# A hybrid decoder block: a fourth pair of the gate/up product by seven products, SiLU in one activation, unsplit feed-forward blocks

## The chip, the cores and the metric

The kernel runs on one core of one Trainium2 chip. The metric is the device time of one execution in microseconds (us), lower is better. TensorE (PE) multiplies, VectorE (DVE) and ScalarE (ACT) work elementwise, GpSimd (POOL) issues a few DMAs, SyncE (SP) issues the loads of weights.

## The reference

One decoder layer on 256 tokens of width 2048, in float32. The part around the change is the SwiGLU feed-forward:

```python
    x = x + jnp.concatenate([attn_out, mlstm_out], axis=-1) @ w_out[i]
    h2 = rms_norm(x, w_norm_ffn[i])
    x = x + (jax.nn.silu(h2 @ w_ffn_gate[i]) * (h2 @ w_ffn_up[i])) @ w_ffn_down[i]
    gate = jax.nn.sigmoid(rms_norm(x, w_norm_ple[i]) @ w_ple_gate[i])
    e = rms_norm(p[i] @ w_ple_proj[i], w_ple_post_norm[i])
    x = x + gate * e
```

Ahead of it stand attention and an mLSTM with their projections. The feed-forward is 5632 wide.

## The kernel before

Every float32 product is made of three: both factors are split into a high part (`h`, rounded to the matmul's format) and a low part (`l`, what is left), and h·h, h·l and l·h are added up in PSUM. `halves` splits weights: ACT writes the high part (`wh`, line 219), DVE subtracts (`wl`, line 220). On a tile of 128x1024 elements each is one instruction.

The gate and up projections run over 11 columns of 512 features (`gate_up`). A column needs the 256 tokens (two blocks of 128) times 16 blocks of the inner dimension, taken as eight pairs. For one pair, token blocks x inner blocks and inner blocks x (gate, up) are two 2x2 matrices of blocks, so a pair is eight block products (`plain_unit`, 24 matmuls) or, by the scheme of Strassen and Winograd, seven (`seven_unit`, 21 matmuls). Seven products need sums of blocks: DVE makes four sums of weights per pair (`wt`, lines 731 to 735), and these are split too (`th`, `tl`; the same two lines 219 and 220). The sums of token blocks are made once for each pair (`make_forms`, tiles `fh`, `fl`). The tuple `seven` names the pairs done so, `later_order` the order of the eight pairs in columns 1 to 10. Column 0 has a tuple and an order of its own.

At a column's end eight additions on DVE (lines 780 to 789) combine the banks of PSUM; then comes SiLU: ACT takes a sigmoid (line 793), DVE multiplies twice (lines 794, 795). `after_up` turns the block round: DVE transposes 32x32 pieces (line 187), POOL sends it to memory and back (`swap`, `quad`), and ACT copies it out. The blocks of columns 0 to 3 are split there at once into a high and a low part (lines 129, 130); those of columns 4 to 10 are kept in float32 (line 668) and split by `split_raw` each time that the down projection (`linear` on `w_down`, four columns of 512, called from `residual`) comes to one.

The order of instructions on each engine is that of a scheduler, which moves them within the order of the code by its own estimate. An engine works its list off in order. Loads of weights go through SP into four buffers `wr`; `wh` and `wl` have four buffers each, `wt`, `th` and `tl` two.

Of the kernel before, what the change touches and what calls it, by code (L numbers as in the profile page):

```python
# [14 lines left out]
P = 128  # L15
# [4 lines left out]
def block_kernel(ctx, tc, x, p, w_norm_mix, w_in, fox_f_bias, q_norm_w, k_norm_w, conv_w, conv_b,  # L20
# [202 lines left out]
    def linear(w, acts, c0, n, pieces=None, before=None, load=None, width=2, split_raw=None):  # L223

        acts = list(acts)
        po = [ps.tile([P, 512], F32, name=f"acc{b}") for b in range(2)]
        total = w.shape[0] // P
        if pieces is None:
            step = 1024 // n if n < 512 else 2
            pieces = [(k, min(step, total - k)) for k in range(0, total, step)]  # L230
        count = 0
        ready = []

        def fetch(i):
            kt, nk = pieces[i]
            if load is not None:
                load(kt)

            ready.append(halves(load_piece(w, kt, nk, c0, n)))

        for i, (kt, nk) in enumerate(pieces):
            if before is None:
                advance(width)
                fetch(i)
            else:
                if i == 0:
                    fetch(0)
                    before(kt)
                if i + 1 < len(pieces):
                    fetch(i + 1)  # L250
                if i:
                    before(kt)
            wh, wl = ready[i]
            for j in range(nk):
                ah, al = acts[(kt + j) // 4]
                while id(ah) in made_by and not made_by[id(ah)].done:
                    advance(2)
                if al is None:
                    ah, al = acts[(kt + j) // 4] = split_raw(ah)
                kk = (kt + j) % 4  # L260
                count += 1
                for b in range(2):
                    s = slice(b * P, (b + 1) * P)
                    nc.tensor.matmul(po[b][:, 0:n], ah[:, kk, s], wh[:, j, :], start=count == 1, stop=False)  # L264
                    nc.tensor.matmul(po[b][:, 0:n], ah[:, kk, s], wl[:, j, :], start=False, stop=False)  # L265
                    nc.tensor.matmul(po[b][:, 0:n], al[:, kk, s], wh[:, j, :], start=False, stop=count == total)  # L266
        return [t[:, 0:n] for t in po]


# [389 lines left out]
    with tc.tile_pool(name="ffnp", bufs=1) as fp:  # L659
        acts_g = []  # L660

        def after_up(dst, gg):
            if dst[1] is not None:
                yield from split_by_blocks(dst, lambda b: gg[b])
                return
            tv = yield from transposed(lambda b: gg[b])
            for k in range(0, 4, 2):
                nc.scalar.copy(dst[0][:, k:k + 2].rearrange("p k (t r) -> p k t r", r=32), tv[:, k:k + 2])
                if not k:
                    yield  # L670
            held.pop()
# [7 lines left out]

        first_seven, seven = (1, 2), (1, 2, 4)
        first_order, later_order = (0, 3, 4, 1, 5, 2, 6, 7), (0, 3, 1, 5, 2, 6, 4, 7)
        forms = {}

        def make_forms(p):
# [58 lines left out]
        def gate_up(c):  # L745

            own, shared = (("acc0", "acc1"), ("tr", "sc"))[::1 - 2 * (c % 2)]
            tags = {"P1": own[0], "P6": own[0], "P7": own[1], "P5": own[1],
                    "P2": shared[0], "P3": shared[1], "P4": shared[0], "P8": shared[1]}
            order, by_seven = (later_order, seven) if c else (first_order, first_seven)  # L750
            n7 = len(by_seven)
            left = {**{n: n7 for n in ("P1", "P6", "P7", "P5")}, **{n: 16 - n7 for n in ("P2", "P3", "P4")}, "P8": 16 - 2 * n7}
            bank, t1, qr, su = {}, None, None, None
            for p in order:
                advance(1)
                if p in by_seven:
                    while p not in forms:
                        advance(1)
                    unit = seven_unit(c, p)
                else:  # L760
                    h = acts_h[p // 2]
                    unit = plain_unit(c, p, h)
                    while id(h[0]) in made_by and not made_by[id(h[0])].done:
                        advance(2)
                advance(1)
                for n, (lh, ll), (rh, rl) in unit:
                    first = n not in bank
                    if first:
                        bank[n] = ps.tile([P, 512], F32, name=tags[n])
                    left[n] -= 1  # L770
                    nc.tensor.matmul(bank[n], lh, rh, start=first, stop=False)  # L771
                    nc.tensor.matmul(bank[n], lh, rl, start=False, stop=False)  # L772
                    nc.tensor.matmul(bank[n], ll, rh, start=False, stop=left[n] == 0)  # L773
                if su is None and left["P1"] == 0:
                    while held:
                        advance(1)
                    t1 = fp.tile([P, 512], F32, name="sg", bufs=2)
                    nc.scalar.copy(t1, bank["P1"])
                    qr = quads.tile([P, 2, 512], F32, name="quad")
                    nc.vector.tensor_tensor(qr[:, 0], bank["P6"], t1, op=ALU.add)  # L780
                    nc.vector.tensor_tensor(qr[:, 1], bank["P7"], qr[:, 0], op=ALU.add)
                    su = quads.tile([P, 2, 512], F32, name="tq")
                    for i in range(2):
                        nc.vector.tensor_tensor(su[:, i], bank["P5"], qr[:, i], op=ALU.add)
            gg = [fp.tile([P, 512], F32, name=f"gg{b}") for b in range(2)]
            nc.vector.tensor_tensor(gg[0], bank["P2"], t1, op=ALU.add)
            nc.vector.tensor_tensor(gg[1], bank["P4"], qr[:, 1], op=ALU.add)
            nc.vector.tensor_tensor(su[:, 0], bank["P3"], su[:, 0], op=ALU.add)
            nc.vector.tensor_tensor(su[:, 1], bank["P8"], su[:, 1], op=ALU.add)
            for b in range(2):  # L790
                r = rstd2[:, b:b + 1]
                sg = fp.tile([P, 512], F32, name="sg", bufs=2)
                nc.scalar.activation(sg, gg[b], AF.Sigmoid, scale=r)
                nc.vector.scalar_tensor_tensor(gg[b], gg[b], r, sg, op0=ALU.mult, op1=ALU.mult)
                nc.vector.scalar_tensor_tensor(gg[b], su[:, b], r, gg[b], op0=ALU.mult, op1=ALU.mult)
            return gg

        for c in range(NG):
# [1 line left out]
                Task(make_forms(kp), [made_by[id(acts_h[kp // 2][0])]])  # L800
            gg = gate_up(c)
            if c < 4:
                acts_g.append(new_act())
            else:
                acts_g.append((fp.tile([P, 4, 256], F32, name=f"g{c}"), None))
            made_by[id(acts_g[c][0])] = Task(after_up(acts_g[c], gg))
# [84 lines left out]
```

## Time and profile before

| | |
|---|---|
| time, median of 3 runs | 1218.33 us (1216.01 to 1219.6) |
| the profiled execution's own time | 1218.38 us |
| its span from the first to the last instruction | 1216.6 us |
| PE busy | 1201.3 us, 99% of the span |
| DVE busy | 918.6 us, 76% |
| ACT busy | 669.1 us, 55% |

Busy times of PE overlap one another, since matmuls are pipelined: what one matmul takes is read from the distance between two starts, not from its own duration. The same holds, to a smaller degree, for DVE.

### The profile page before, as it was taken

The page shows a single profiled execution, that of the slowest core. Times are in us where ns is not written, and L with a number is a line of the kernel's source. Part 1 is how long each engine was busy: PE and PEld are TensorE (multiplying, and loading weights), DVE is VectorE, ACT ScalarE, POOL GpSimd, SP SyncE. Part 2 cuts the span into 40 slices and gives each one's busy share as a digit, 9 for nine tenths or more (in the row PEclk, how much of TensorE's full clock was granted, in tenths as well). Part 3 has the DMA queues.
Part 4 walks back from the last instruction along what each step waited for, and adds up shares of the span by engine and source line. Part 5 has one row for each costly group of instructions (what it writes and reads, how often), then busy time and mean ns, then how long its engine had stood idle before and what let it go on. Part 6 is the DMA issues. An engine that isn't in the chain of part 4 may idle for free.

```text
span 1216.6 us, 15632 instructions
## 1 busy us (share of the span) xinstructions
PE 1201.3 (99%) x5579; PEld 999.1 (82%) x5579; DVE 918.6 (76%) x1270; ACT 669.1 (55%) x884; POOL 79.7 (7%) x149
## 2 busy tenths in 40 slices
PE   9999999999999999999999999999999999999998
PEld 6899978888888787787788878887788888888888
DVE  5767755656656999899999999998965757565854
ACT  6655556547545646455555555565554645456542
POOL 1111000001010000000000000000000000000000
PEclk9999999999999999999999999999999999999999
DMA  7677744676577676676776777676676666664772
GB/s 262 208 237 234 239 139 125 185 231 191 190 246 238 200 226 198 225 232 192 235 232 202 245 217 231 204 251 216 210 249 207 207 211 206 218 209 161 236 229 88
DMA packets 136386, 257.33 MB, mean 212 GB/s; under 512 B 10003, under 2 KB 29301, under 8 KB 136309
## 3 DMA queue, kind: packets, MB, share of 16 engines
q1 hardware_dynamic: 127156, 229.06, 59.2%
q0 software_dynamic: 8400, 26.22, 6.8%
q8 instruction: 43, 0.70, 0.2%
q10 hardware_dynamic: 752, 1.06, 0.2%
q14 instruction: 35, 0.28, 0.1%
HBM read 241.10 MB, written 15.20 MB: 211 GB/s over the span
## 4 chain that ended last, share of the span: by engine, by line
PE 83%; DVE 6%; DMA 6%; issue 2%; ACT 1%; POOL 1%; SPq 0%; DVEq 0%; POOLq 0%; ACTq 0%
PE acc L265 18%; PE acc L266 18%; PE acc L264 18%; PE acc L772 5%; PE acc L773 5%; PE acc L771 5%; DMA quad<-swap 3%; DMA swap<-tq 2%; PE tr L772 2%; PE tr L773 2%; PE tr L771 2%; PE sc L772 2%; PE sc L773 2%; PE sc L771 2%; DVE wl L220 2%
## 5 line engine op out<-in xcount | busy, mean ns | idle before, releaser
L220 DVE TENSOR_TENSOR wl<-wr,wh 128x1024 fp32r<-128x1024 f32 (+2 forms) x445 | 504.4, 1142 | 189.8 <-ACT wh L219 188.8
L219 ACT CAST wh<-wr 128x1024 fp32r<-128x1024 f32 (+2 forms) x445 | 433.8, 986 | 330.5 <-PE acc L266 204.2
L264 PE MATMUL acc<-wh,act_h 128*128 128x512 f32 (+2 forms) x864 | 320.1, 371 | 0.6 <-ACT act_h L133 0.5
L266 PE MATMUL acc<-wh,act_l 128*128 128x512 f32 (+2 forms) x864 | 318.0, 368 | 0.0
L265 PE MATMUL acc<-wl,act_h 128*128 128x512 f32 (+2 forms) x864 | 317.5, 368 | 0.4 <-DVE wl L220 0.4
L264 PEld LDWEIGHTS acc<-wh,act_h 128*128 128x128 f32 x864 | 162.8, 188 | 24.9 <-ACT act_h L133 1.3
L266 PEld LDWEIGHTS acc<-wh,act_l 128*128 128x128 f32 x864 | 162.7, 188 | 24.5 <-DVE act_l L135 0.8
L265 PEld LDWEIGHTS acc<-wl,act_h 128*128 128x128 f32 x864 | 162.9, 189 | 23.6 <-DVE wl L220 0.9
L191 POOL DMA_DIRECT2D swap<-tq x100 | 61.2, 618 | 867.5 <-DVE tq L187 832.1
L219 ACT CAST th<-wt 128x1024 fp32r<-128x1024 f32 x64 | 67.2, 1051 | 72.2 <-DVE wt L732 63.4
L771 PE MATMUL acc<-wh,act_h 128*128 128x512 f32 x232 | 90.3, 390 | 0.7 <-ACT wh L219 0.7
L773 PE MATMUL acc<-wh,act_l 128*128 128x512 f32 x232 | 90.6, 390 | 0.0
L772 PE MATMUL acc<-wl,act_h 128*128 128x512 f32 x232 | 90.5, 390 | 0.0
L266 PE MATMUL acc<-wh,tl 128*128 128x512 f32 x224 | 87.2, 390 | 1.1 <-DVE tl L220 1.1
L265 PE MATMUL acc<-wl,th 128*128 128x512 f32 x224 | 88.1, 393 | 0.0
L264 PE MATMUL acc<-wh,th 128*128 128x512 f32 x224 | 87.9, 393 | 0.0
L220 DVE TENSOR_TENSOR tl<-wt,th 128x1024 fp32r<-128x1024 f32 x64 | 78.0, 1221 | 5.2 <-ACT th L219 4.9
L772 PE MATMUL tr<-wl,act_h 128*128 128x512 f32 x156 | 61.0, 391 | 0.6 <-DVE wl L220 0.6
L773 PE MATMUL tr<-wh,act_l 128*128 128x512 f32 x156 | 61.0, 391 | 0.0
L771 PE MATMUL tr<-wh,act_h 128*128 128x512 f32 x156 | 60.6, 390 | 0.0
L220 DVE TENSOR_TENSOR tl<-g,th 128x1024 fp32r<-128x1024 f32 x28 | 34.3, 1223 | 24.5 <-ACT th L219 24.4
L771 PEld LDWEIGHTS acc<-wh,act_h 128*128 128x128 f32 x232 | 43.6, 188 | 10.4 <-ACT wh L219 1.1
(285 smaller groups left out, 1495.9 us busy)
## 6 DMA issues: line engine op xcount, KB each, us to landing
wr<-in_w_ffn_gate_dram SPq DMA_DIRECT2D x88, 512.0 KB, 3.5
wr<-in_w_ffn_up_dram SPq DMA_DIRECT2D x88, 512.0 KB, 4.6
wr<-in_w_ffn_down_dram SPq DMA_DIRECT2D x88, 512.0 KB, 4.7
wr<-in_w_in_dram SPq DMA_DIRECT2D x63, 512.0 KB, 4.8
wr<-in_w_in_dram SPq DMA_DIRECT2D x48, 344.0 KB, 3.9
wr<-in_w_out_dram SPq DMA_DIRECT2D x32, 512.0 KB, 4.1
wr<-in_w_ple_gate_dram SPq DMA_DIRECT2D x32, 512.0 KB, 4.5
swap<-tq POOLq DMA_DIRECT2D x100, 128.0 KB, 3.8
```

The source lines that it names most:

```text
L191: nc.gpsimd.dma_start(out=d[:, :, :, i, :].rearrange("j c b e -> c b j e"), in_=t[32 * i:32 * i + 32].rearrange("c b j k r -> c b j (k r)"))
L219: nc.scalar.copy(wh, wr)
L220: nc.vector.tensor_tensor(wl, wr, wh.bitcast(F32), op=ALU.subtract)
L264: nc.tensor.matmul(po[b][:, 0:n], ah[:, kk, s], wh[:, j, :], start=count == 1, stop=False)
L265: nc.tensor.matmul(po[b][:, 0:n], ah[:, kk, s], wl[:, j, :], start=False, stop=False)
L266: nc.tensor.matmul(po[b][:, 0:n], al[:, kk, s], wh[:, j, :], start=False, stop=count == total)
L771: nc.tensor.matmul(bank[n], lh, rh, start=first, stop=False)
L772: nc.tensor.matmul(bank[n], lh, rl, start=False, stop=False)
L773: nc.tensor.matmul(bank[n], ll, rh, start=False, stop=left[n] == 0)
```

## The change

There are three edits and a new order. Pair 5 joins the pairs done by seven products in columns 1 to 10, and the order of the pairs there becomes 0, 1, 3, 2, 4, 6, 5, 7. ACT computes SiLU itself, and one multiplication on DVE goes. The blocks of columns 0 to 3 stay in float32 as the others do, so that the down projection splits all eleven each time it comes to them. For that, `linear` gets the function `ahead`, which issues the split of the next group of four blocks one group early, and `after_up` waits three steps of background work, not two, between its transfers.

```diff
     def linear(w, acts, c0, n, pieces=None, before=None, load=None, width=2, split_raw=None):
         acts = list(acts)
+
+        def ahead(k):
+
+            raw = acts[k // 4][0]
+            if acts[k // 4][1] is None and (id(raw) not in made_by or made_by[id(raw)].done):
+                acts[k // 4] = split_raw(raw)
+
...
+            if split_raw is not None and kt % 4 == 0 and i + 2 < len(pieces):
+                ahead(pieces[i + 2][0])
         return [t[:, 0:n] for t in po]
...
         def after_up(dst, gg):
-            if dst[1] is not None:
-                yield from split_by_blocks(dst, lambda b: gg[b])
-                return
-            tv = yield from transposed(lambda b: gg[b])
+            tv = yield from transposed(lambda b: gg[b], 3)
...
-        first_seven, seven = (1, 2), (1, 2, 4)
-        first_order, later_order = (0, 3, 4, 1, 5, 2, 6, 7), (0, 3, 1, 5, 2, 6, 4, 7)
+        first_seven, seven = (1, 2), (1, 2, 4, 5)
+        first_order, later_order = (0, 3, 4, 1, 5, 2, 6, 7), (0, 1, 3, 2, 4, 6, 5, 7)
...
                 sg = fp.tile([P, 512], F32, name="sg", bufs=2)
-                nc.scalar.activation(sg, gg[b], AF.Sigmoid, scale=r)
-                nc.vector.scalar_tensor_tensor(gg[b], gg[b], r, sg, op0=ALU.mult, op1=ALU.mult)
-                nc.vector.scalar_tensor_tensor(gg[b], su[:, b], r, gg[b], op0=ALU.mult, op1=ALU.mult)
+                nc.scalar.activation(sg, gg[b], AF.Silu, scale=r)
+                nc.vector.scalar_tensor_tensor(gg[b], su[:, b], r, sg, op0=ALU.mult, op1=ALU.mult)
...
-                acts_g.append(new_act())
+                acts_g.append((act.tile([P, 4, 256], F32, name="act_h"), None))
```

The lists of instructions change in three places that the prediction speaks of. The line numbers of the changed kernel are higher by 6 or 5 in these places.

The first is DVE in the last pairs of column 3 (`wr` is a loaded piece of weights). Before, the last pair by seven products is pair 4, and the plain pairs 6 and 7 stand round it as `wl` rows:

```order
L220 TENSOR_TENSOR tl<-wt,th 128x1024 x2
L220 TENSOR_TENSOR wl<-wr,wh 128x1024 x2
L731 TENSOR_TENSOR wt<-wr 128x512
L220 TENSOR_TENSOR wl<-wr,wh 128x1024
L732 TENSOR_TENSOR wt<-wt,wr 128x512
L220 TENSOR_TENSOR wl<-wr,wh 128x512
L734 TENSOR_TENSOR wt<-wt,wr 128x512
L735 TENSOR_TENSOR wt<-wr,wt 128x512
```

After the change pair 5 stands there, right ahead of the column's sums, and pair 4 two pairs earlier:

```order
L220 TENSOR_TENSOR wl<-wr,wh 128x1024 x3
L737 TENSOR_TENSOR wt<-wr 128x512
L220 TENSOR_TENSOR wl<-wr,wh 128x512
L738 TENSOR_TENSOR wt<-wt,wr 128x512
L740 TENSOR_TENSOR wt<-wt,wr 128x512
L741 TENSOR_TENSOR wt<-wr,wt 128x512
L220 TENSOR_TENSOR tl<-wt,th 128x1024
L220 TENSOR_TENSOR wl<-wr,wh 128x1024
L220 TENSOR_TENSOR tl<-wt,th 128x1024
L786 TENSOR_TENSOR quad<-tr,sg 128x512
```

Pair 5, which was two `wl` rows on 128x1024, is now one such row, one on 128x512, four `wt` rows and two `tl` rows.

The second is DVE at the end of column 3, where `gg` is the block that SiLU makes. Before:

```order
L786 TENSOR_TENSOR gg_5239<-acc_4908,sg 128x512
L788 TENSOR_TENSOR tq<-acc_4912,tq 128x512
L787 TENSOR_TENSOR gg_5240<-acc_4916,quad 128x512
L794 SCALAR_TENSOR_TENSOR gg_5239<-gg_5239,rstd_ffn,sg 128x512
L789 TENSOR_TENSOR tq<-acc_4920,tq 128x512
L795 SCALAR_TENSOR_TENSOR gg_5239<-tq,rstd_ffn,gg_5239 128x512
L794 SCALAR_TENSOR_TENSOR gg_5240<-gg_5240,rstd_ffn,sg 128x512
L220 TENSOR_TENSOR wl<-wr,wh 128x1024
L795 SCALAR_TENSOR_TENSOR gg_5240<-tq,rstd_ffn,gg_5240 128x512
```

And now:

```order
L792 TENSOR_TENSOR gg_5268<-acc_4928,sg 128x512
L794 TENSOR_TENSOR tq<-acc_4932,tq 128x512
L793 TENSOR_TENSOR gg_5269<-acc_4936,quad 128x512
L795 TENSOR_TENSOR tq<-acc_4940,tq 128x512
L800 SCALAR_TENSOR_TENSOR gg_5268<-tq,rstd_ffn,sg 128x512
L800 SCALAR_TENSOR_TENSOR gg_5269<-tq,rstd_ffn,sg 128x512
L220 TENSOR_TENSOR wl<-wr,wh 128x1024
```

Two of the four multiplications are gone.

The third is DVE where the last column ends and the down projection begins (`g_5620` and `g_5653` are the same block, that of column 4, with which it begins). Before, its first split stands among the column's sums:

```order
L780 TENSOR_TENSOR quad<-acc_7558,sg 128x512
L220 TENSOR_TENSOR tl<-g_5620,th 128x1024
L781 TENSOR_TENSOR quad<-acc_7569,quad 128x512
L784 TENSOR_TENSOR tq<-acc_7562,quad 128x512 x2
L220 TENSOR_TENSOR wl<-wr,wh 128x1024 x2
L786 TENSOR_TENSOR gg_7790<-tr,sg 128x512
```

Now it stands behind them:

```order
L792 TENSOR_TENSOR gg_7879<-tr,sg 128x512
L794 TENSOR_TENSOR tq<-sc,tq 128x512
L793 TENSOR_TENSOR gg_7880<-tr,quad 128x512
L795 TENSOR_TENSOR tq<-sc,tq 128x512
L800 SCALAR_TENSOR_TENSOR gg_7879<-tq,rstd_ffn,sg 128x512
L800 SCALAR_TENSOR_TENSOR gg_7880<-tq,rstd_ffn,sg 128x512
L220 TENSOR_TENSOR tl<-g_5653,th 128x1024
L187 STREAM_TRANSPOSE tq<-gg_7879 128x512
L187 STREAM_TRANSPOSE tq<-gg_7880 128x512
L220 TENSOR_TENSOR tl<-g_6026,th 128x1024
L220 TENSOR_TENSOR wl<-wr,wh 128x1024 x4
```

The first `tl` moved from ahead of the eight sums' second half to behind both multiplications, and the weights of the second piece (`wl` x4) stand behind the transposes.

## Rows read from the trace of the kernel before

**Rows 1.** The page: busy time per engine, and DVE's busy tenths in 40 slices.

```profile
PE 1201.3 (99%) x5579; PEld 999.1 (82%) x5579; DVE 918.6 (76%) x1270; ACT 669.1 (55%) x884; POOL 79.7 (7%) x149
DVE  5767755656656999899999999998965757565854
```

**Rows 2.** Busy time by stretch: columns 1, 2, 5 and 10, cut at their second sigmoid.

```profile
core 0: us, PE busy (x) PEld busy (x) DVE busy (x) ACT busy (x) POOL busy (x), PEclk, DMA share, GB/s
440.63:482.82 42.19, 42.19 (x184) 34.00 (x184) 41.56 (x56) 24.27 (x29) 2.99 (x5) 1.00 0.69 217
482.82:528.84 46.02, 42.87 (x185) 34.03 (x184) 42.31 (x52) 24.00 (x28) 2.99 (x5) 1.00 0.67 215
...
615.81:657.72 41.91, 41.91 (x185) 34.29 (x184) 39.93 (x49) 23.84 (x28) 2.98 (x5) 1.00 0.72 226
...
826.16:870.22 44.06, 43.29 (x188) 34.78 (x187) 40.73 (x50) 25.46 (x31) 2.99 (x5) 1.00 0.64 207
```

**Rows 3.** Timeline of PE in column 5; start and duration in us come first.

```profile
640.04 0.39 PE L771 MATMUL acc<-th,act_h 128*128 128x512 f32 x1
...
641.44 0.39 PE L771 MATMUL acc<-wh,act_h 128*128 128x512 f32 x1
...
644.18 0.39 PE L771 MATMUL acc<-wh,act_h 128*128 128x512 f32 x1
...
646.90 0.39 PE L771 MATMUL tr<-wh,act_h 128*128 128x512 f32 x1
```

**Rows 4.** Timeline of DVE in column 6, its second pair by seven products.

```profile
671.59 1.22 DVE L220 TENSOR_TENSOR wl<-wr,wh 128x1024 fp32r<-128x1024 f32 x1
674.21 0.69 DVE L731 TENSOR_TENSOR wt<-wr 128x512 f32<-128x512 f32 x1 [1.41 <-DMA wr<-in_w_ffn_up_dram]
674.82 1.22 DVE L220 TENSOR_TENSOR wl<-wr,wh 128x1024 fp32r<-128x1024 f32 x1
675.96 0.69 DVE L732 TENSOR_TENSOR wt<-wt,wr 128x512 f32<-128x512 f32 x1
676.56 0.69 DVE L220 TENSOR_TENSOR wl<-wr,wh 128x512 fp32r<-128x512 f32 x1
```

**Rows 5.** Timeline of DVE at the end of column 3.

```profile
564.38 0.68 DVE L780 TENSOR_TENSOR quad<-tr,sg 128x512 f32<-128x512 f32 x1
565.16 0.69 DVE L781 TENSOR_TENSOR quad<-sc,quad 128x512 f32<-128x512 f32 x1
...
569.90 0.69 DVE L786 TENSOR_TENSOR gg<-acc,sg 128x512 f32<-128x512 f32 x1 [0.59 <-PE acc L773]
...
571.87 0.74 DVE L794 SCALAR_TENSOR_TENSOR gg<-gg,rstd_ffn,sg 128x512 f32<-128x512 f32 x1
572.53 0.69 DVE L789 TENSOR_TENSOR tq<-acc,tq 128x512 f32<-128x512 f32 x1
```

**Rows 6.** Waits: who waited for whom, us in total, times, longest.

```profile
DVE wt L731 <- DMA wr<-in_w_ffn_up_dram: 9.0, 11, 1.5
```

**Rows 7.** Groups by line and shape: busy us, mean ns, idle before.

```profile
L794 DVE SCALAR_TENSOR_TENSOR gg<-gg,rstd_ffn,sg 128x512 f32<-128x512 f32 x22 | 16.2, 745 | 0.0
...
L609 ACT ACT_TABLE_LOAD x3 | 3.8, 1283 | 0.1
```

**Rows 8.** Timeline of DVE in column 0: two of a form's four small sums.

```profile
419.94 0.29 DVE L701 SCALAR_TENSOR_TENSOR quad<-tq 128x128 f32<-128x128 f32 x1
420.14 0.28 DVE L703 TENSOR_TENSOR quad<-tq 128x128 f32<-128x128 f32 x1
```

**Rows 9.** Timeline of ACT: the first sigmoid of the feed-forward, the first of the last stage.

```profile
439.06 0.72 ACT L793 ACTIVATE sg<-gg,rstd_ffn 128x512 f32<-128x512 f32 x1 [1.89 <-DVE gg L786]
...
1144.91 1.37 ACT L859 ACTIVATE gg<-acc,rstd_ple 128x512 f32<-128x512 f32 x2 [0.99 <-PE acc L266]
```

**Rows 10.** Timeline of PE in the down projection: a wait at its start, and blocks split there.

```profile
876.57 0.73 PE L266 MATMUL acc<-wh,tl 128*128 128x512 f32 x2 [1.06 <-DVE tl L220]
...
901.85 0.40 PE L264 MATMUL acc<-wh,th 128*128 128x512 f32 x1
...
903.91 0.40 PE L264 MATMUL acc<-wh,th 128*128 128x512 f32 x1
```

## The prediction

> **What bounds the kernel now.** I read the page first. PE is busy for 99% of the span, which says little by itself, since matmuls overlap; but DVE's line has a run of 9s in the middle, about the fourteen slices of the gate and up projections, and nowhere else [rows 1]. So that stage has two engines near their limit, and the change moves work between just these two.
>
> Next come the stretches, one for each column. The ten columns 1 to 10 take from 440.63 to 870.22, that is 429.59 us, 42.96 each. An undisturbed one takes 41.91 with PE busy throughout, and column 2 takes 46.02 with PE idle for 3 us of it [rows 2]. The granted clock is 1.00 everywhere, so clock plays no part.
>
> The pace is in the starts of PE's matmuls: twelve of a plain pair in 646.90 - 644.18 = 2.72 us, 0.2267 each, and six of a pair by seven products in 1.40 us, 0.2333 each [rows 3]. A column has five plain pairs of 24 and three of 21: 120 x 0.2267 + 63 x 0.2333 = 41.9 us. That is the 41.91 measured. An undisturbed column runs at PE's pace with nothing over.
>
> DVE's pace comes from its starts in the same way. Instructions on 1024 elements follow each other after 1.14 us and those on 512 after 0.60 [rows 4], the multiplications after 0.66 [rows 5]. A pair by seven products has three of the long kind and five short: 3 x 1.14 + 5 x 0.60 = 6.42 us. A plain pair has two long: 2.28. A column before: 3 x 6.42 + 5 x 2.28, eight sums (4.80), four multiplications (2.64), two transposes (1.20 at the short pace): 39.3 us. The second of the eight sums starts 0.78 after the first, not 0.60, because it reads the first's result [rows 5]: 39.5. DVE thus has 2.4 us to spare in a column of 41.91. It waits in that time: once a column, at its second pair by seven products, for weights to land (1.41 in column 6; 9.0 us in 11 waits, 0.82 each) [rows 4, 6], and at the column's end for PE [rows 5].
>
> **The change part by part.** *PE.* Pair 5 loses three matmuls and its other 21 take the slower pace: 96 x 0.2267 + 84 x 0.2333 = 41.4 us, 0.5 less per column. That is all the change can bring where PE sets the pace.
>
> *DVE, seven products.* 6.42 in place of 2.28: +4.14 per column. *DVE, SiLU.* Two multiplications fewer: -1.32 per column (22 in all, [rows 7]). Sum: 39.3 + 4.1 - 1.3 = 42.1, and 42.3 with the 0.18 above. That is more than PE's 41.4, and more than the 41.91 of an undisturbed column before. DVE becomes the engine that sets the pace.
>
> *The wait for weights.* The second pair's loads go into the buffers that the first pair's last sums free; between lie, before and after, the same four long instructions on DVE. Before, DVE had time for that wait. Now it costs its full 0.82 per column. Bounds: nothing, if loads land sooner, to the 1.5 of the longest such wait [rows 6]. I take the mean: it is the same load behind the same cover. 42.3 + 0.8 = 43.1 per column, 431 for ten.
>
> *Forms.* Column 1 now makes the forms of pairs 4 and 5, each four small sums at 0.20 [rows 8] and two short instructions: 2.0 us, so 4.0. Against that, the lists show the second weight piece of column 1's first pair split before the column begins: -1.1. Ten columns: 431 + 2.9 = 433.9, against 429.6: **+4.3**.
>
> *Unsplit blocks.* In columns 1 to 4 two short subtractions go, 1.2 us each; they are not in the 42.3. They are what column 2 stumbled over, so the 4.1 us that it takes above 41.91 [rows 2] is before's loss and not after's; the sum has that, since it sets whole columns against whole columns. In return the down projection splits four more blocks in each of its four columns, 16 x 1.14 on DVE and as many casts on ACT. A group there lasts 24 matmuls, 5.5 us, for three long instructions, 3.4: hidden. If that cover were gone it would be 18 us. PE's pace with blocks split there is 2.06 / 9 = 0.2289 [rows 10] against 0.2267 [rows 3]; 4 x 96 matmuls change over: **+0.8**.
>
> *The start of the down projection.* In the new list the first split stands behind four sums and two multiplications: 2.4 + 1.3 + 1.2 = 4.9 us after the column's last sums begin. PE is done with the column some 1.6 us after that point (the last sum, 1.8 us in, needs its result), has four matmuls that need no low part (0.9), and waits 2.4. It then has ten matmuls (2.3, to 7.2), and the second piece's weights, behind two transposes and another split, come at 8.4: 1.2 more. Before, PE waited 1.06 there [rows 10]. **+2.5**. Bounds: 0 to 2.5.
>
> *ACT.* Pair 5 adds one and a half casts per column to an engine busy for 24 of 42 us [rows 2]: hidden. That SiLU takes what the sigmoid takes (0.72 as a row, [rows 9]) no row shows; at twice that, DVE would wait about 0.7 per column, +7 us, and below the sigmoid there is nothing to gain, as ACT idles ahead of it. I take equal. The lists show two more loads of ACT's tables, one before the first SiLU and one before the last stage's sigmoid. A load is 1.28 us [rows 7]; ACT idles 1.89 and 0.99 at the two places [rows 9]: at most 0.3 shows, and PE has weights in hand there: 0. The Trainium skill (ScalarE: Activation LUTs, What ACT_TABLE_LOAD costs, and Table sets: the hidden batching unit) says to batch activations by table set, and counts 2.66 us per switch with its drain. By that the two gaps would be outlasted by 0.8 and 1.7 us, +2.5 at most; no row here shows the drain.
>
> Sum: 4.3 + 0.8 + 2.5 = +7.6 on the profiled execution's own 1218.38: **1226 us**. That execution stands at the median of the three runs, 1218.33.
>
> **The rivals.** *PE keeps the pace (faster).* If DVE keeps up, ten columns of 41.4 and column 1's forms hidden make 414, -15.6, and with +0.8 and half the start's cost 1205. For it: each edit but one relieves DVE, and 9s in the page leave the true load open. Against it: the count of 42.3 uses distances between starts, which hide nothing. It decides when a long instruction follows in less than 1.14 x 41.4 / 42.3 = 1.11 us, or when DVE works well ahead over the plain pairs. The Trainium skill (Perfetto Trace Analysis, Engine Utilization) gives VectorE a peak of 245.76 G elements/s in float32. By that rule a long instruction would take 0.53 us, DVE would be half idle and this rival would win; the trace disagrees, with 1.14 [rows 4]. Chance 0.17.
>
> *DVE sets the pace but waits for nothing (about the same).* 10 x 42.3 + 2.9 = 425.9, -3.7, with the down projection's 0.8 and a hidden start: 1215.5; with the start's cost 1218. For it: a load that waits for a slower DVE may meet less traffic. Against it: ten columns of before had the wait. Chance 0.20.
>
> *Lockstep (much slower).* With DVE and PE within 1 us of each other, each late low part stops PE, and PE's late last product stops DVE's sums at the column's end, where it already waits 0.59 [rows 5]. Column 2 lost 4.1 in this manner and column 10 2.1 [rows 2]. One more us in each column gives 1236; it decides if PE comes to the column's last product later than DVE to its sums. Chance 0.15.
>
> **How the numbers follow.** The forecast, 1220 to 1231, has 0.48. About 0.3%, or 3.7 us, is what a measurement of this kernel can tell from no change. Faster by more: the first rival and a third of the second, 0.24. Within: the rest of the second and the low end of the forecast (wait 0.5, start hidden), 0.26. Slower: 0.50. The range leaves out most of the first rival and the far end of the third: 1211 to 1236.
>
> **What would show it.** Right: columns 2 to 10 at 42.5 to 44 us, all alike; DVE without a gap in them except the wait for weights at the second pair by seven products, about 0.8; PE's gaps as waits for `wl` and `tl`, 1.5 us or more per column; column 1 at 45; a PE wait of 2 us or more for `tl` at the start of the down projection, and none later. Wrong: columns under 42 with PE full (first rival); columns at 42.3 and no wait (second); DVE waiting for PE or for SiLU at each column's end (third, or a longer SiLU); a PE gap in the down projection each time a block is split.

## The result, and the profile after

The changed kernel takes 1234.85 us (median of 4 runs, 1234.23 to 1236.09), the kernel before 1217.17 beside it (1215.96 to 1219.6): 1.0143 times as long, 95% interval 1.0122 to 1.0164. The profiled execution spans 1234.4 us, 17.8 more than before's 1216.6.

The page of the changed kernel, its busy times and DVE's tenths (answers to [rows 1]):

```profile
PE 1212.6 (98%) x5549; PEld 988.5 (80%) x5549; DVE 960.8 (78%) x1322; ACT 700.3 (57%) x923; POOL 79.7 (6%) x149
DVE  5767756656666989999999999999967677776754
```

DVE has 52 instructions more, PE 30 matmuls fewer. DVE's 9s now run through columns 2 to 10 without a break.

Busy time by stretch, cut at the columns' second SiLU: columns 1 and 2, and all nine of columns 2 to 10 as one stretch (the figures of a line stand in the order of [rows 2]):

```profile
439.75:485.95 46.20, 43.26 (x180) 32.84 (x179) 43.97 (x62) 27.55 (x32) 2.99 (x5) 1.00 0.57 182
485.95:530.82 44.87, 43.19 (x181) 32.62 (x180) 43.44 (x54) 25.20 (x31) 2.99 (x5) 1.00 0.70 221
...
485.95:883.53 397.58, 387.58 (x1621) 296.93 (x1620) 384.82 (x470) 227.97 (x264) 26.92 (x45) 1.00 0.68 216
```

Column 1 takes 46.20 us, columns 2 to 10 take 397.58 / 9 = 44.18 each, from 43.49 to 45.02. The ten together take 883.53 - 439.75 = 443.78, where before had 429.59: +14.2. Column 0 ends 0.9 earlier (439.75 against 440.63). What follows takes 1234.4 - 883.53 = 350.87 against 1216.6 - 870.22 = 346.38: +4.5. Together +17.8, the whole difference.

The waits of DVE in columns 2 to 10 (who waited for whom: us in all, times, longest), as in [rows 6]:

```profile
DVE wt L737 <- DMA wr<-in_w_ffn_up_dram: 10.9, 13, 1.4
DVE wl L220 <- ACT wh L219: 0.7, 1, 0.7
```

And one of these waits in column 7, with the load that it waits for, on the timelines of SP's queue and of DVE (as in [rows 4]):

```profile
714.90 0.37 SPq L212 DMA_DIRECT2D wr<-in_w_ffn_up_dram  x1
```

```profile
718.19 1.23 DVE L220 TENSOR_TENSOR wl<-wr,wh 128x1024 fp32r<-128x1024 f32 x1
720.71 0.69 DVE L737 TENSOR_TENSOR wt<-wr 128x512 f32<-128x512 f32 x1 [1.30 <-DMA wr<-in_w_ffn_up_dram]
```

The load is issued at 714.90, when the first pair's last sum has freed the buffer, and the wait for it ends 5.8 us later; DVE has work until 719.42, and its next instruction starts 1.30 after that. Without a wait it would have started 1.14 after 718.19, that is at 719.33: the wait costs the column 1.38, because the overlap of two neighbours is lost too. Of the 13 waits nine stand at pair 2, one in each column, and four at pair 5.

PE at the start of the down projection (as in [rows 10]):

```profile
883.74 0.40 PE L272 MATMUL acc<-wl,th 128*128 128x512 f32 x1
886.46 0.96 PE L273 MATMUL acc<-wh,tl 128*128 128x512 f32 x2 [2.32 <-DVE tl L220]
887.22 0.63 PE L271 MATMUL acc<-wh,th 128*128 128x512 f32 x1
887.64 0.63 PE L272 MATMUL acc<-wl,th 128*128 128x512 f32 x1
...
889.77 0.83 PE L271 MATMUL acc<-wh,th 128*128 128x512 f32 x2
```

The granted clock in these stretches (the last three columns of a line: PEclk, share of DMA, GB/s):

```profile
887.30:890.20 2.90, 2.90 (x8) 2.23 (x7) 2.90 (x4) 0.14 (x1) 2.17 (x4) 0.50 0.72 228
890.20:894.00 3.80, 3.80 (x20) 3.11 (x19) 3.07 (x3) 1.81 (x2) 0.27 (x1) 1.00 0.85 224
```

PE stood from one start to the next for 886.46 - 883.74 = 2.72 us, and then ran at a granted clock of 0.50, the lower of TensorE's two levels (1.2 GHz): starts 0.42 apart instead of 0.23. From 890.20 on the clock is back at 1.00.

### The profile page after: what moved, and what is told of

Same layout as the page of the kernel before. It is cut to its first block, busy times and chain, and to the rows that moved or that the text cites. A ratio compares the mean times of both kernels' runs of the same rounds, so it can differ in the third digit from the quotient of the medians.

```text
span 1234.4 us, 15747 instructions
## 1 busy us (share of the span) xinstructions
PE 1212.6 (98%) x5549; PEld 988.5 (80%) x5549; DVE 960.8 (78%) x1322; ACT 700.3 (57%) x923; POOL 79.7 (6%) x149
## 3 DMA queue, kind: packets, MB, share of 16 engines
q10 hardware_dynamic: 752, 1.06, 0.2%
## 4 chain that ended last, share of the span: by engine, by line
PE 72%; DVE 14%; DMA 7%; issue 4%; ACT 2%; SPq 0%; DVEq 0%; ACTq 0%
PE acc L272 19%; PE acc L271 19%; PE acc L273 19%; DMA wr<-in_w_ffn_up_dram 5%; DVE wl L220 4%; PE acc L778 2%; PE acc L779 2%; PE acc L777 2%; DVE tl L220 2%; DMA wr<-in_w_ffn_gate_dram 2%; DVE wt L737 2%; DVE wt L738 1%; PE sc L778 1%; DVE wt L741 1%; PE sc L779 1%
## 5 line engine op out<-in xcount | busy, mean ns | idle before, releaser
L271 PE MATMUL acc<-wh,act_h 128*128 128x512 f32 (+2 forms) x736 | 270.0, 367 | 0.0
L273 PE MATMUL acc<-wh,act_l 128*128 128x512 f32 (+2 forms) x736 | 267.7, 364 | 0.0
L272 PE MATMUL acc<-wl,act_h 128*128 128x512 f32 (+2 forms) x736 | 267.2, 363 | 0.4 <-DVE wl L220 0.4
L271 PEld LDWEIGHTS acc<-wh,act_h 128*128 128x128 f32 x736 | 138.6, 188 | 19.1 <-ACT act_h L133 0.6
L273 PE MATMUL acc<-wh,tl 128*128 128x512 f32 x352 | 137.3, 390 | 2.3 <-DVE tl L220 2.3
L272 PE MATMUL acc<-wl,th 128*128 128x512 f32 x352 | 139.2, 396 | 0.0
L271 PE MATMUL acc<-wh,th 128*128 128x512 f32 x352 | 138.6, 394 | 0.0
L220 DVE TENSOR_TENSOR tl<-wt,th 128x1024 fp32r<-128x1024 f32 x84 | 101.7, 1220 | 1.0 <-ACT th L219 0.9
L273 PEld LDWEIGHTS acc<-wh,tl 128*128 128x128 f32 x352 | 66.3, 189 | 17.5 <-DVE tl L220 2.8
L271 PEld LDWEIGHTS acc<-wh,th 128*128 128x128 f32 x352 | 66.6, 189 | 15.7
L272 PEld LDWEIGHTS acc<-wl,th 128*128 128x128 f32 x352 | 66.5, 189 | 13.2
```

Of the source, the lines that this page charges most:

```text
L220: nc.vector.tensor_tensor(wl, wr, wh.bitcast(F32), op=ALU.subtract)
```

## The experiments

Three theories were to be told apart: DVE's work sets the pace of the columns and its own waits add to it (the forecast); DVE and PE run in lockstep and pass lateness on to each other; PE still sets the pace. Where a line number is given it is that of the changed kernel or shifted by a few.

**Three pairs, with the rest of the change.**

```diff
-        first_seven, seven = (1, 2), (1, 2, 4, 5)
-        first_order, later_order = (0, 3, 4, 1, 5, 2, 6, 7), (0, 1, 3, 2, 4, 6, 5, 7)
+        first_seven, seven = (1, 2), (1, 2, 4)
+        first_order, later_order = (0, 3, 4, 1, 5, 2, 6, 7), (0, 3, 1, 5, 2, 6, 4, 7)
```

> The changed kernel with pairs 1, 2 and 4 alone by seven products and the order of pairs of before; SiLU in one activation, the unsplit blocks and the early splits stay. Theory (DVE's work sets the columns' pace in the changed kernel, 42.1 us of it against PE's 41.4): DVE falls to 38.0 us per column, PE sets the pace again at 41.9 us, the stumble of column 2 over the split of a block does not come back: 1208 to 1217 us. Rival (SiLU, the unsplit blocks or the early splits cost the time, not the fourth pair): 1225 us or more.

Measured 1207.58 us (1207.19 to 1208.95), 0.9907 times the kernel before (0.9884 to 0.993): just under the theory's range, and faster than both kernels. Columns 2 to 10 of this run in one stretch:

```profile
482.85:858.74 375.89, 375.89 (x1649) 308.99 (x1648) 349.17 (x416) 215.79 (x247) 26.92 (x45) 1.00 0.73 226
```

41.77 each, with PE busy in all of it: with 4.1 us less on DVE, PE sets the pace and nothing shows but its own matmuls. The fourth pair with its order is what costs the time, 27 us of it.

**The fourth pair and its order alone**, in the kernel before.

```diff
-        first_seven, seven = (1, 2), (1, 2, 4)
-        first_order, later_order = (0, 3, 4, 1, 5, 2, 6, 7), (0, 3, 1, 5, 2, 6, 4, 7)
+        first_seven, seven = (1, 2), (1, 2, 4, 5)
+        first_order, later_order = (0, 3, 4, 1, 5, 2, 6, 7), (0, 1, 3, 2, 4, 6, 5, 7)
```

> The kernel before with the fourth pair and the new order of pairs, and nothing else: sigmoid and two multiplications, blocks 0 to 3 split at once. Theory (DVE's work sets the pace): 1.3 us more of DVE work in each of ten columns and 1.2 us more in four than in the changed kernel, so 1235 + 13 + 5 less the later start of the down projection, 1247 to 1256 us. Rival (waits for weights and for PE set the pace, and DVE's work fits beside them): 1232 to 1240 us.

Measured 1256.14 us (1254.83 to 1259.23), ratio 1.0305 (1.0281 to 1.0329): at the upper end of the theory's range. Columns 2 to 10 take 412.29 us, 45.81 each, 1.63 more than in the changed kernel; the two multiplications that SiLU saves are 1.32 of that, and the blocks split in columns 2 to 4 (two subtractions of 0.6 us each) would account for the rest.

**SiLU alone**, in the kernel before.

```diff
-                nc.scalar.activation(sg, gg[b], AF.Sigmoid, scale=r)
-                nc.vector.scalar_tensor_tensor(gg[b], gg[b], r, sg, op0=ALU.mult, op1=ALU.mult)
-                nc.vector.scalar_tensor_tensor(gg[b], su[:, b], r, gg[b], op0=ALU.mult, op1=ALU.mult)
+                nc.scalar.activation(sg, gg[b], AF.Silu, scale=r)
+                nc.vector.scalar_tensor_tensor(gg[b], su[:, b], r, sg, op0=ALU.mult, op1=ALU.mult)
```

> The kernel before with SiLU in one activation and nothing else changed: DVE loses 1.3 us of work per column. Theory (in the kernel before PE sets the pace of an undisturbed column and only columns 2, 3, 4 and 10 are late, by some 9 us in all, for DVE's sake): a part of that lateness goes, columns 5 to 9 stay at 41.8 to 42.2, time 1211 to 1217. Rival 1 (SiLU takes longer on ScalarE than the sigmoid, or its table loads show): no gain or a loss, 1219 to 1227, with DVE waiting for the activation at each column's end. Rival 2 (all that DVE saves shows): 13 us less, 1204 to 1208.

Measured 1209.75 us (1208.67 to 1211.49), ratio 0.9932 (0.9911 to 0.9953), a little better than the theory's range. Columns 2 to 10:

```profile
483.52:861.30 377.78, 376.40 (x1649) 308.84 (x1648) 352.68 (x422) 216.34 (x247) 26.92 (x45) 1.00 0.73 226
```

41.98 each, 9.6 us less in all than before's 387.40 (482.82 to 870.22 [rows 2]), for 9 x 1.32 = 11.9 us less work on DVE. So most of what DVE saved came through, PE is busy in all but 1.4 us of the stretch, and no table load shows.

**Unsplit blocks alone**, in the kernel before (`ahead` is defined as in the change).

```diff
...
+            if split_raw is not None and kt % 4 == 0 and i + 2 < len(pieces):
+                ahead(pieces[i + 2][0])
...
-            if dst[1] is not None:
-                yield from split_by_blocks(dst, lambda b: gg[b])
-                return
-            tv = yield from transposed(lambda b: gg[b])
+            tv = yield from transposed(lambda b: gg[b], 3)
...
-                acts_g.append(new_act())
+                acts_g.append((act.tile([P, 4, 256], F32, name="act_h"), None))
```

> The kernel before with all feed-forward blocks kept unsplit (and the split one group ahead in the down projection, and three steps between the transfers) and nothing else changed. Theory (the split of a block in columns 1 to 4 is what column 2 and its neighbours stumble over; the splits in the down projection are hidden but for 0.8 us of PE's pace): columns 2 to 4 fall to 42 to 43 us, the rest stays, time 1211 to 1216. Rival (the sixteen added splits show in the down projection, or the stumble has another cause): 1218 or more.

Measured 1214.65 us (1211.68 to 1218.0), ratio 0.9967 (0.9949 to 0.9985): the theory in the time and in columns 2 to 4. Column 2 fell from 46.02 [rows 2] to 42.95:

```profile
483.53:526.48 42.95, 42.14 (x184) 33.82 (x183) 39.84 (x49) 23.90 (x29) 2.98 (x5) 1.00 0.72 226
```

But what follows the columns takes 1213.3 - 863.86 = 349.4 us here, 3.0 more than before where 0.8 was expected, and the added splits show in it, as the rival had it: PE waits for both halves of one split block, and the two starts come 0.66 and 0.92 us after those before them, 1.1 more than twice a matmul's 0.23:

```profile
887.20 0.50 PE L271 MATMUL acc<-wh,th 128*128 128x512 f32 x1 [0.26 <-ACT th L219]
...
888.46 0.50 PE L273 MATMUL acc<-wh,tl 128*128 128x512 f32 x1 [0.52 <-DVE tl L220]
```

The changed kernel has no such wait behind the start of the down projection.

The two edits alone give 8.8 and 3.9 us by their medians, and 11.8 together in the run with three pairs.

**One sum less, one sum more on DVE.** The fourth sum of weights of each pair, left out or made twice:

```diff
-            nc.vector.tensor_tensor(t34[:, 1], ra[:, 1], t12[:, 1], op=ALU.subtract)
+            nc.scalar.copy(t34[:, 1], ra[:, 1])
```

> The changed kernel with the fourth sum of weights of each pair by seven products left out (ScalarE copies the loaded block in its place, so the product P4 has a wrong factor): DVE loses four short instructions per column, 4 x 0.60 = 2.4 us, PE has the same work. Theory (DVE's work and its own waits set the pace of columns 2 to 10, 42.1 + 2 us): columns fall by 2.2 to 2.4 us to 41.8 to 42.2, where PE's 41.4 is next, time 1211 to 1216. Rival (what was added to the columns is waiting between DVE, PE and ScalarE, not DVE's work): columns stay over 43 us, time 1222 or more.

```diff
             nc.vector.tensor_tensor(t34[:, 1], ra[:, 1], t12[:, 1], op=ALU.subtract)
+            nc.vector.tensor_tensor(t34[:, 1], ra[:, 1], t12[:, 1], op=ALU.subtract)
```

> The changed kernel with the fourth sum of weights of each pair by seven products made twice: DVE gains four short instructions per column, 2.4 us, and 25 us over all columns. Theory (DVE's work sets the pace): each microsecond added shows as one, columns at 46.4 to 46.8 us, time 1257 to 1262. Rival 1 (DVE takes the place of its waits: it is not the bound): under 1250. Rival 2 (each further late low part makes PE and ScalarE late in turn): over 1266.

Measured: one less 1219.9 us (1218.64 to 1221.29), ratio 1.0027 (1.0014 to 1.0039); one more 1266.85 us (1265.13 to 1270.28), ratio 1.0415 (1.0392 to 1.0439). The time of the first came out between theory and rival, its columns (43.04) just inside the rival; the second came out just inside its second rival. Columns 2 to 10, first with one sum less, then with one more:

```profile
483.63:870.98 387.35, 378.61 (x1624) 300.90 (x1623) 367.55 (x436) 246.69 (x301) 27.00 (x45) 1.00 0.68 221
```

```profile
491.22:917.96 426.74, 397.44 (x1614) 296.81 (x1613) 401.95 (x505) 231.00 (x265) 27.00 (x45) 0.99 0.63 200
```

Beside the 397.58 of the changed kernel, 21.6 us less work on DVE (36 sums of 0.60) saved 10.2 us, and 21.6 more cost 29.2. DVE's work does come through, but not one to one. With one sum less DVE's count is 42.1 - 2.4 = 39.7 us, 1.7 under PE's 41.4, and still the columns take 43.04: there, neither engine's own work fills the column, and waits make up the rest. With less of it the waits for ScalarE's high parts grew, to 7.7 us; ScalarE has four copies more per column in that run, so it is not DVE's saving alone. With more of it the waits for weights grew from 10.9 to 17.2 us:

```profile
DVE tl L220 <- ACT th L219: 4.3, 10, 0.7
DVE wl L220 <- ACT wh L219: 3.4, 8, 1.1
```

```profile
DVE wt L737 <- DMA wr<-in_w_ffn_up_dram: 17.2, 8, 4.0
```

**Less work on PE.**

```diff
-                    nc.tensor.matmul(bank[n], lh, rl, start=False, stop=False)
+                    if not c or p not in (6, 7):
+                        nc.tensor.matmul(bank[n], lh, rl, start=False, stop=False)
```

> The changed kernel with the high-by-low product left out in pairs 6 and 7 of columns 1 to 10: PE loses 16 matmuls per column, 3.6 us of 41.4, DVE has the same work. Theory (DVE sets the pace; of its waits only the 0.3 us per column for PE's last products hangs on PE): columns at 43.6 to 44.2 us, time 1228 to 1234. Rival (lockstep: PE is within 1 us of DVE, so each saving on PE comes through in part): columns at 43 us or less, time 1223 or less.

Measured 1241.72 us (1240.35 to 1242.85), ratio 1.0202 (1.0184 to 1.0219): over both ranges. Columns 2 to 10:

```profile
485.54:886.95 401.41, 367.87 (x1474) 287.33 (x1473) 382.13 (x469) 230.65 (x265) 27.00 (x45) 0.94 0.68 213
```

44.60 each although PE lost 3.6 us of work per column. That contradicts "PE keeps the pace": PE was busy for 367.87 of 401.41 us. For lockstep the run is not a clean test, since PE's granted clock had a mean of 0.94 in this stretch and took back a part of what PE had saved. That the columns became 0.4 longer was not expected. DVE's waits for ScalarE rose from 0.7 us to 10.3, and ScalarE's own waits for PE from 16.8 us to 51.0, nearly all of it in two lines:

```profile
ACT wh L219 <- PE tr L780: 25.3, 21, 2.3
ACT wh L219 <- PE acc L780: 24.8, 10, 6.3
```

So lateness of PE can reach DVE by way of ScalarE; that the slower clock is what made PE late here is argued, not shown.

**A fifth buffer for loaded weights**, with the up piece of a pair by seven products loaded ahead of its gate piece.

```diff
...
+        loads = [0]
+
+        def ring():
+            loads[0] += 1
+            if loads[0] % 5 == 0:
+                return fp.tile([P, 1024], F32, name="wr5")
+            return wpool.tile([P, 1024], F32, name="wr")
...
-            w2 = [halves(load_piece(w, 2 * p, 2, c * 512, 512)) for w in (w_gate, w_up)]
+            w2 = [halves(load_piece(w, 2 * p, 2, c * 512, 512, ring)) for w in (w_gate, w_up)]
...
-            ra, rb = (load_piece(w, 2 * p, 2, c * 512, 512) for w in (w_gate, w_up))
+            rb, ra = (load_piece(w, 2 * p, 2, c * 512, 512, ring) for w in (w_up, w_gate))
```

> The changed kernel with a fifth buffer for loaded weights in the ten columns (every fifth load goes into a buffer of its own), and the up piece of a pair by seven products loaded ahead of its gate piece. Theory (DVE sets the pace, and its wait for weights at the second pair by seven products, 12.0 us in 13 waits over columns 2 to 10, adds to each column): the wait goes, columns fall from 44.2 to about 43 us, time 1221 to 1226. Rival (DVE and PE run in lockstep, and time taken from one wait comes back at the next one): DVE's wait for weights goes from the trace, but columns stay at 43.8 or more, with longer waits for PE or for ScalarE in its place, time 1231 to 1236.

Measured 1237.52 us (1235.53 to 1238.35), ratio 1.0156 (1.0124 to 1.0189). The theory missed; the rival holds in the columns (43.83 each) and is 1.5 us too low in the time, because columns 0 and 1 came 4.2 us later. DVE's waits in columns 2 to 10:

```profile
DVE wt L744 <- DMA wr<-in_w_ffn_gate_dram: 4.1, 4, 1.3
DVE tl L220 <- ACT th L219: 2.8, 4, 1.5
DVE wl L220 <- ACT wh L219: 2.2, 7, 0.4
```

The wait for weights fell from 10.9 us to 4.1, and 5.0 us of waits for ScalarE (0.7 in the changed kernel) took much of its place. So the wait for weights is where lateness shows, not the only thing that makes it: ScalarE, which casts what has just landed, is late next.

**Two plain pairs ahead of the second pair by seven products.**

```diff
-        ..., (0, 1, 3, 2, 4, 6, 5, 7)
+        ..., (0, 1, 3, 6, 2, 4, 5, 7)
```

> The changed kernel with the order 0, 1, 3, 6, 2, 4, 5, 7, so that two plain pairs and not one stand between the first and the second pair by seven products. Theory (of the columns' 44.2 us, 42.1 are DVE's work and 1.3 its wait for the weights of the second such pair): that wait goes, columns take 42.6 to 43.2 us, 1222 to 1228 us in all. Rival (the wait only changes its place, to the third or fourth pair or to PE at the column's end): 1232 to 1240 us.

Measured 1271.57 us (1270.17 to 1274.53), ratio 1.0431 (1.0407 to 1.0455): far over both. The timeline of DVE and that of SP's queue at the place where the wait was to go:

```profile
596.26 1.22 DVE L220 TENSOR_TENSOR wl<-wr,wh 128x1024 fp32r<-128x1024 f32 x1
597.65 2.51 DVE L220 TENSOR_TENSOR wl<-wr,wh 128x1024 fp32r<-128x1024 f32 x2 [0.17 <-ACT wh L219]
604.50 0.69 DVE L737 TENSOR_TENSOR wt<-wr 128x512 f32<-128x512 f32 x1 [4.35 <-DMA wr<-in_w_ffn_up_dram]
```

```profile
597.54 0.37 SPq L212 DMA_DIRECT2D wr<-in_w_ffn_up_dram  x1
```

Four buffers hold two pairs, so the loads of pair 2 go into the buffers of pair 3, two pairs ahead. The one that DVE waits for is issued at 597.54, right after DVE's last instruction on pair 3 ends (596.26 + 1.22 = 597.48), and the wait for it ends 7.0 us later. Between lies pair 6 alone, a plain pair: 2.5 us of work on DVE. A plain pair gives DVE 2.28 us of work per two loads, a pair by seven products 6.42. In the changed kernel the buffers come from pair 1, and its own last low parts stand behind their release too: four long instructions in all, not two. So a second plain pair is not more cover for a load but less.

**The fourth sum on GpSimd.**

```diff
-            nc.vector.tensor_tensor(t34[:, 1], ra[:, 1], t12[:, 1], op=ALU.subtract)
+            nc.gpsimd.tensor_tensor(out=t34[:, 1], in0=ra[:, 1], in1=t12[:, 1], op=ALU.subtract)
```

> The changed kernel with one of the four weight sums of each pair by seven products (the last, the second half of the second tile) on GpSimd. Theory (DVE's work sets the pace): DVE loses 0.6 us per such pair, 2.4 per column, so 39.7 us, less than PE's 41.4; columns at 42 to 43 us, 1212 to 1222 us in all. Rival (the sums' chain to the low part is what counts): GpSimd takes 1 us or more for the sum, the cast and the last low part of each such pair come later, and columns stay at 44 us or grow: 1232 to 1260 us.

Measured 1294.89 us (1286.13 to 1297.94), ratio 1.0607 (1.0564 to 1.0651). The theory fell; the rival's direction holds, 35 us above its range. Two sums on POOL, and what stood beside them on DVE:

```profile
624.18 2.25 POOL L741 TENSOR_TENSOR wt<-wr,wt 128x512 f32<-128x512 f32 x1 [5.82 <-DVE wt L738]
...
644.30 1.30 POOL L741 TENSOR_TENSOR wt<-wr,wt 128x512 f32<-128x512 f32 x1
```

```profile
625.24 2.27 DVE L220 TENSOR_TENSOR tl<-wt,th 128x1024 fp32r<-128x1024 f32 x1
627.43 1.21 DVE L220 TENSOR_TENSOR wl<-wr,wh 128x1024 fp32r<-128x1024 f32 x1
...
643.90 2.79 DVE L220 TENSOR_TENSOR tl<-wt,th 128x1024 fp32r<-128x1024 f32 x1 [0.18 <-ACT th L219]
```

The two long instructions on DVE took 2.27 and 2.79 us where 1.22 is usual, and both ended 1.1 us after POOL's sum beside them (627.51 after 626.43, 646.69 after 645.60). Over the columns the low parts `tl` took 1.43 us on average (1.22 in the changed kernel), and the third sum, on DVE beside POOL's, 1.24 (0.69). Each pair thus loses 2 x 0.21 + 0.55 = 0.97 us of DVE's time where the moved sum saves 0.60.

**An earlier first split for the down projection.** The split of the first block stands ahead of the last pair of the last column.

```diff
...
             for p in order:
+                if c == NG - 1 and p == order[-1]:
+                    first_split.append(split_raw(acts_g[4][0]))
                 advance(1)
```

> The changed kernel with the split of the first block of the down projection moved ahead of the last column's last pair in the code, which puts it on DVE among the column's sums instead of behind the multiplications. Theory (PE waits 2.7 us at the start of the down projection for this split, and after that wait the granted clock falls and nine matmuls take 0.43 us each, some 2 us more): both go, the ten matmuls run at 0.23, time 1230.5 to 1232.5. Rival (the split, 1.1 us ahead of the column's end on DVE, delays the last sums by as much, and PE waits for the next pieces instead): 1233.5 to 1236, and the clock falls all the same.

Measured 1238.23 us (1236.85 to 1241.48), ratio 1.0168 (1.0126 to 1.0209). The rival's mechanism holds, 2 us above its range:

```profile
885.54 0.63 PE L271 MATMUL acc<-wh,th 128*128 128x512 f32 x2
888.95 0.80 PE L272 MATMUL acc<-wl,th 128*128 128x512 f32 x1 [2.78 <-DVE wl L220]
```

```profile
888.95:892.00 3.05, 3.05 (x7) 2.47 (x8) 3.05 (x4) 0.00 (x0) 1.48 (x3) 0.50 0.87 232
```

PE waits 3.2 us from start to start, now for the low part of weights, and then runs at a granted clock of 0.50 again. DVE has too much to do ahead of this point; in which order it does it changes only the name of the wait.

**Three pairs in the last column alone.**

```diff
             n7 = len(by_seven)
+            if c == NG - 1:
+                order, by_seven = (0, 3, 1, 5, 2, 6, 4, 7), (1, 2, 4)
```

> The changed kernel with three pairs by seven products in the order of the kernel before in the last column alone (pair 5 plain there): DVE loses 4.1 us of work ahead of the down projection, which itself stays as it is. Theory (PE's wait of 2.7 us at the start of the down projection is DVE's lateness at the end of the last column, and the slower matmuls behind it follow from that wait): the last column falls from 44.2 to 42.0 to 43 us, PE's wait at the start falls under 0.8 us, no matmul there takes 0.43 us, and the rest after the columns falls from 350.9 to 346.8 to 347.6; time 1228 to 1231. Rival (the wait is made by the down projection's own order of loads and splits): the last column gains its 1 to 2 us, the rest after the columns stays within a microsecond of 350.9, time 1232 to 1234.

Measured 1229.17 us (1228.92 to 1229.66), ratio 1.0091 (1.0061 to 1.0122): the theory, with the rest 0.1 us below its range. PE goes from the column into the down projection and over its first low part without a stop, and one later distance of 0.45 is a wait for weights:

```profile
879.73 0.39 PE L781 MATMUL sc<-wh,act_l 128*128 128x512 f32 x1
879.96 0.39 PE L271 MATMUL acc<-wh,th 128*128 128x512 f32 x1
...
880.42 0.39 PE L273 MATMUL acc<-wh,tl 128*128 128x512 f32 x1
```

The granted clock stays at 1.00. The last column takes 880.67 - 837.69 = 42.98 us, and what follows 1227.4 - 880.67 = 346.7.

## Why the prediction held, point by point

The sign, the engine and the places were right. The time lies in the range, but 9 us above the forecast and outside its own 1220 to 1231: it is the room given to the third rival, up to 1236, that holds it, and by the number alone that rival came nearer. The two traces' spans differ by 17.8 where the sum had 7.6. Nearly all of the missing 10.2 lies in one term, the columns (+14.2 for +4.3).

- *DVE's work per column.* Right. Three pairs instead of four bring the columns down to PE's pace, and 3.6 us less on PE, at a lower clock, did not bring them down. The distances between starts count 42.1 us of DVE's work in a column, as forecast.
- *The wait for weights.* Mis-sized: 0.82 per column, and 1.34 came. The mean of one wait was right, 10.9 / 13 = 0.84. But there were 13 in nine columns, since pair 5 waits in four of them as pair 2 does in all (in the new order 4, 6, 5 stand as 1, 3, 2 do, and the prediction looked at pair 2 alone), and each also loses the 0.09 by which neighbours overlap: (10.9 + 13 x 0.09) / 9 = 1.34. The bound of 1.5 held it. The up pieces, for which DVE waits, took no longer from issue to landing than before; only the gate pieces did. Medians in columns 2 to 10, first before, then after (KB each, us):

```profile
wr<-in_w_ffn_up_dram SPq DMA_DIRECT2D x70, 512.0 KB, 4.7
wr<-in_w_ffn_gate_dram SPq DMA_DIRECT2D x69, 512.0 KB, 3.5
```

```profile
wr<-in_w_ffn_gate_dram SPq DMA_DIRECT2D x70, 512.0 KB, 4.9
wr<-in_w_ffn_up_dram SPq DMA_DIRECT2D x70, 512.0 KB, 4.8
```

- *Nothing else in a column.* This step failed. The forecast had DVE without a gap but for that wait. From the distances between its starts DVE also lost about 0.3 us per column at the column's end, where its last sums start 0.68 apart and not 0.60 (three of PE's matmuls take 0.68; the profile names PE for a part of this loss only), and 0.1 to 0.2 for ScalarE's casts. In column 10:

```profile
882.58 0.69 DVE L793 TENSOR_TENSOR gg<-tr,quad 128x512 f32<-128x512 f32 x1
883.26 0.69 DVE L795 TENSOR_TENSOR tq<-sc,tq 128x512 f32<-128x512 f32 x1
```

  With the 0.5 above that is about 1.0 of the 1.1 by which columns 2 to 10 (44.18) exceed the forecast's 43.1. This is the size of the lockstep rival, one more us in each column, which gave 1236. Its mechanism is at least a part of it: DVE does wait for PE at the column's end. Less work on PE did not help, but at the lower clock of that run this does not rule the rest out. Which of these waits is a cause and which only the place where lateness shows, no run settled; those with one sum less, one sum more and a fifth buffer say that they trade places, and that a microsecond of DVE's work is worth from half a microsecond to 1.35.
- *Column 1.* 46.0 was forecast (43.1 and 2.9 for the forms), 46.2 came; the 45 among the prediction's signs does not fit its own sum.
- *The signs.* Columns 2 to 10 were to take 42.5 to 44 us; six of the nine take more. PE's gaps were to be waits for `wl` and `tl`: PE did lose 44.18 - 41.4 = 2.8 us per column, but of its waits that the profile names, 8.4 us in the nine columns, 4.5 are for ScalarE's `th`, which in turn waits for DVE's sums, 0.7 for `wh`, and only 3.2 for `tl` and `wl`. The wait at the start of the down projection, and none later, held.
- *Unsplit blocks.* Right: alone they take column 2 from 46.0 to 42.95. In the changed kernel the sixteen splits in the down projection stay hidden; with unsplit blocks alone two waits for them, 1.1 us, do show. With three pairs in the last column the rest takes 346.7 us against 346.38 before, with before's wait of 1.23 (1.46 from start to start, that is 1.06 idle [rows 10] behind a matmul of 0.40, less a matmul's 0.23) gone: 1.6 us more in this part, of which 0.8 was forecast and the other 0.8 is not explained.
- *The start of the down projection.* Mis-sized: +2.5 forecast, and given as the upper bound too. PE's wait came as predicted (2.72 from start to start, 2.49 lost, where before lost 1.23). The second wait, 1.2 for the next piece's weights, never showed, because the ten matmuls ahead of it took 890.45 - 886.46 = 3.99 us at the lower clock instead of 2.3. Against the run with three pairs in the last column the start costs 350.87 - 346.7 = 4.2: 2.5 of waiting and 1.7 of slow clock. The clock was in no step of the prediction, and the second wait only happened not to come: its place was taken by slow matmuls that cost more.
- *SiLU and the tables.* Right: no cost. An activation takes 0.72, as the sigmoid did [rows 9], and the first table load, 1.28 us, ends ahead of the first SiLU, which then waits for DVE. The second stands right between a cast, which starts at 1160.62 and takes 1.06, and the last stage's sigmoid:

```profile
435.29 1.28 ACT L799 ACT_TABLE_LOAD   x1
437.52 0.73 ACT L799 ACTIVATE sg<-gg,rstd_ffn 128x512 f32<-128x512 f32 x1 [0.95 <-DVE gg L792]
```

```profile
1161.69 1.28 ACT L864 ACT_TABLE_LOAD   x1
1162.99 1.27 ACT L864 ACTIVATE gg<-acc,rstd_ple 128x512 f32<-128x512 f32 x2
```

The Trainium skill (ScalarE: Activation LUTs, What ACT_TABLE_LOAD costs) counts 2.66 us per switch, the load and a drain together; the trace disagrees, with 1162.99 - 1161.68 = 1.31 from the end of that cast to the start of the sigmoid, and at the first SiLU 0.95 to spare behind the load.

- *The rivals.* "PE keeps the pace" fell in the changed kernel and is what three pairs do. "DVE waits for nothing" fell with the thirteen waits. Lockstep as the source of the last microsecond is neither shown nor excluded.

## What to carry to other kernels

Count an engine's work by the distances between its starts before moving work to it. Here DVE's count went from 2.4 us under PE's to 0.7 over it, and its waits, until then free, were paid in full; at 1.7 under it they still were in part. So count the waits by place and number, not by their mean, and expect that removing one uncovers the next. A change of several edits is worth taking apart: here two of three give 1% and the third takes more than 2%. Cover for a load is the work of the engine that frees its buffer, so work that uses buffers up quickly is little cover.

## What the runs showed of the hardware

- In the 2.72 us from 883.74 to 886.46 PE started nothing; then the granted clock was 0.50, and ten matmuls took 3.99 us before it was back at 1.00. In the run with an earlier split 3.2 us without a start were followed by a clock of 0.50 too. Before's 1.46 us at the same place were followed by 1.00:

```profile
876.57:880.00 3.43, 3.43 (x15) 2.85 (x16) 3.43 (x4) 1.06 (x1) 1.68 (x3) 1.00 1.06 285
```

- A subtraction of 128x512 in float32 is on record with 2.2 us on average on GpSimd beside a busy DVE (93.1 us for 42, 1.30 in the second row shown), where DVE takes 0.69. The Trainium skill (SBUF — State Buffer, SBUF: two separate sides) says that a GpSimd instruction that reads SBUF and a VectorE instruction with two inputs from SBUF exclude each other for the whole instruction. The trace agrees in the two pairs of rows shown: DVE's instruction ends 1.1 us, nearly its usual length, after POOL's. In the second pair it had even started 0.40 ahead of POOL's.
